# A hybrid mixer's weights split on ScalarE and VectorE instead of by an accumulating DMA, and a longer weight ring in the direct pairs

## The chip, the cores and the metric

One core of a Trainium2 chip runs the whole program. The metric is the device time in microseconds (us) of one execution. A kernel is timed in several executions, and the median counts. One further execution was taken with the hardware profiler, and all rows below are of that one.

## The reference

Two decoder layers over 512 tokens of 1024 features, all in float32. Every layer is a SwiGLU network, a token mixer and another SwiGLU network, each added to the stream; a last RMSNorm ends it. Cut to what the change touches:

```python
def swiglu_ffn(x, g, w_in, w_out):
    h = rms_norm(x, g)
    gate, up = jnp.split(h @ w_in, 2, axis=-1)
    return (jax.nn.silu(gate) * up) @ w_out

def retention_dilated_mixer(x, norm_g, w_in, ret_gn, w_out):      # layer 0: the hybrid mixer
    h = rms_norm(x, norm_g)
    rq, rk, rv, rg, dq, dk, dv = jnp.split(h @ w_in, cuts, axis=-1)
    rq, rk = rotary(rq), rotary(rk)
    ret = merge_heads(head_group_norm(retention_chunkwise(rq, rk, rv), ret_gn)) * jax.nn.silu(rg)
    dil = merge_heads(dilated_attention(rotary(dq), rotary(dk), dv))
    return jnp.concatenate([ret, dil], axis=-1) @ w_out
```

Layer 1 has a stick-breaking attention in the mixer's place. The four networks have an inner width of 2816.

## The kernel before

**Numbers in two parts.** TensorE multiplies in the type fp32r, which rounds. To keep float32's accuracy every operand is cut into a rounded part hi and a remainder lo, and each product is three matmuls (`mm3`, L221): hi by hi, hi by lo, lo by hi. A weight *unit* is a tile of 128 x 1024 floats (512 KB). It comes by DMA into a raw tile (`wraw`), is cut, and hi and lo go into two tiles of a ring (`whl`). One unit of a projection feeds 24 matmuls of 512 columns.

**Two ways to cut a unit.** `weight` (L150) takes hi as a ScalarE cast and lo as a VectorE subtraction, raw minus hi (`split`, L227). `weight_dma` (L196) has ScalarE write minus hi into lo, and then GpSimd's queue issues a DMA that reads the same weights from memory a second time and adds them into lo (`minus_hi`, L191); ScalarE also makes hi. `unit` (L215) takes the second way for the weights in `BY_DMA`, which are all the input weights of the hybrid mixer; the first gate unit alone goes through `weight`. The stick-breaking mixer's weights were cut during earlier stages and kept in memory (`weight_cut`).

**Who sets the order.** Matmuls are chained in the order in which the program calls them (`ordered`, L119). For the other engines a scheduler places each instruction by priority; `tc.high_priority` moves some ahead. Each engine and each DMA queue then works strictly in its order. A tile from a ring can be written once its last reader is done.

**The network.** `ffn_seven` (L551) computes four feature blocks plainly, the *direct pairs*: a gate unit and an up unit each, eight units, of which those of blocks 2 and 3 go through `weight_dma`. Then nine `quad`s follow with seven products in place of eight (L501). Their sums and forms are made by VectorE and ScalarE. `give` sets which slots of memory a role turns through: in the direct pairs before, `wraw` has 4 and `whl` 6, three units; the slots `ext` join for the quads (L598).

**The hybrid mixer** (`hybrid`, L863). Four gate projections come first, into three accumulators in turn. The row factor r of the norm is made from the sum of squares by a matmul `po`, two ScalarE functions and three VectorE steps (`norm_r`, L290); four transposes on TensorE bring it to token order (`token_r`, L623), after the third gate projection before the change. Then a stream of steps (`stream`, L910) makes queries and keys, eight pairs of units, and values, four pairs. A query or key tile is rotated by four VectorE operations (`rot_steps`, L752), cut in two, and moved by DMAs into the layout of the scores (`pack_q`, `pack_k`). Between the steps of the stream the sixteen heads take turns: scores of the next head (`begin`), some steps, then `attend` (L719), whose result ScalarE and VectorE bring out of the bank `po`. After every second retention head `ret_norm` (L809) squares it and a matmul with `bd` sums it. In the mixer before, `wraw` has 2 slots and `whl` 8, four units.

Of the kernel before, what the change touches and what calls it, by code (L numbers as in the profile page):

```python
# [35 lines left out]
def trunk(ctx: ExitStack, tc: tile.TileContext, a: dict, out: bass.AP):  # L36
    nc = tc.nc
# [150 lines left out]

    BY_DMA = ["hyb_" + n for n in ("g", "rq", "rk", "rv", "dq", "dk", "dv")]

    def minus_hi(lo, src, raw):  # L191
# [23 lines left out]
    def unit(key, cols):  # L215
        if key in cut:
            return weight_cut(key, cols)
        src = centred.get(key, array_unit(key))
        return weight_dma(src, cols) if key[0] in BY_DMA else weight(src, cols)

# [330 lines left out]
    def ffn_seven(rms, wd, wq, gcol, first=None):  # L551
# [4 lines left out]
        for i, n in enumerate(("T3", "T1", "T4", "B11", "T2", "B22", "B21")):  # L556
            give(**{"f" + n: forms[2 * i:2 * i + 2]})
        give(uq=late + old[:4])
        uqs = []
        for f in range(DIRECT):  # L560
# [34 lines left out]
            if f == DIRECT - 1:  # L595
                fm = normed_forms(rr, gcol, late[DIRECT // 2 + 1:], forms[12:] + forms[10:12])
        ring = oldest("whl")
        give(wraw=ext[:1] + oldest("wraw") + old[6:], p3=ext[1:2], whl=ring[:4] + ext[2:] + ring[4:] + old[4:6])  # L598
        for q in range((FC - DIRECT) // 2):
# [118 lines left out]

    def attend(v, p, e, banks, o):  # L719

        po = PS("po")
        for j in range(NB):
            b, at = WHERE[e, j]
            n = size(j)
            st = v[j][:, 2 * (p % 2) + e, :, :].rearrange("p a d -> p (a d)")
            for c in range(2):
                mm(po[:, SEQ - n:], st, banks[b][:, c, at:at + n], start=j == 0 and c == 0,
                   stop=j == NB - 1 and c == 1, skip_group_check=True)
        t = T()
        rows, oth = slice(e * DH, e * DH + DH), slice(DH - e * DH, 2 * DH - e * DH)  # L730
        nc.scalar.copy(out=t[rows, :], in_=po[oth, :])
        nc.vector.tensor_add(out=o[rows, :], in0=po[rows, :], in1=t[rows, :])

# [129 lines left out]
    def hybrid(ss, gcol_next):  # L863
        order["on"] = True
        mixer_roles()
        raws, ring = oldest("wraw"), oldest("whl")
        give(wraw=raws[2:], whl=ring + raws[:2])
        gates, held = [], []
        for p in range(4):
            held.append(ACC())  # L870
            if p == 0:
                w = weight(a["hyb_g"][0], D)
                proj_tile(None, held[-1], w)
            else:
                proj_tile(("hyb_g", p), held[-1])
            if p == 0:
                epsr = hpool.tile([P, SEQ], F32, tag="ss", name=nm("epsr"))
                r = norm_r(ss, epsr)
            if p < 2:
                continue  # L880
            if p == 2:
                rtm = token_r(r)
                rtm2 = cpool.tile([P, NB], F32, tag="rtm2", name="rtm2")
                nc.vector.tensor_mul(out=rtm2, in0=rtm, in1=rtm)
                act_set(SILU)
            for ps in held:
                g = T()
                nc.vector.tensor_mul(out=g, in0=ps, in1=r)
                if len(gates) % 2 == 0:
                    gg = B((P, 2, SEQ), F32, f"o{6 + len(gates) // 2}")  # L890
                gates.append(gg[:, len(gates) % 2, :])
                func(gates[-1], g, AF.Silu)
            held = []
# [47 lines left out]
        for h in range(16):  # L941
# [9 lines left out]
            if e == 0:  # L951
                o = T(tag="oo")
            attend(vs[p // 2], p, e, ready.pop(h), o)
            if e == 0:
# [6 lines left out]
        for _ in flow.steps:  # L961
            pass
        raws, ring = oldest("wraw"), oldest("whl")
        give(wraw=raws + ring[:2], whl=ring[2:])
        ss = out_second("hyb_ob", outs, gcol_next)
# [302 lines left out]
```

## Time and profile before

| | us |
|---|---|
| median of 3 runs | 1937.59 |
| lowest, highest | 1937.23, 1941.17 |
| the profiled execution, device time | 1935.8 |
| its span, first to last instruction | 1934.1 |
| TensorE busy with matmuls, in the span | 1908.1 |

The profiled execution's device time is 1.7 us more than its span. In the rows, PE is TensorE's matmuls, PEld its weight loads, DVE VectorE, ACT ScalarE, POOL GpSimd and SP the queue of the plain DMAs. A matmul's listed duration is longer than its share of the engine, because matmuls overlap: the distance from one start to the next tells the pace. An idle time in brackets stands with who ended it; where that engine had long been done, it was another.

### The profile page before, as it was taken

How to read it: one execution, taken by the hardware profiler on the slowest of the kernel's cores; microseconds unless marked ns; L12 is line 12 of the kernel's file. 1: busy time of each engine (PE TensorE's matmuls, PEld its weight loads, DVE VectorE, ACT ScalarE, POOL GpSimd, SP SyncE). 2: the span in 40 equal slices, each digit the busy share in tenths (PEclk: the TensorE clock that was granted, in tenths of full speed). 3: DMA queues.
4: the chain of work that ended last, by engine and by line, in shares of the span. 5: the costliest groups of instructions: out<-in, count | busy, mean ns of one | idle time of the engine just before them, and what ended most of it. 6: DMA issues, size and time to landing. Idle time of an engine off the chain costs nothing.

```text
span 1934.1 us, 30592 instructions
## 1 busy us (share of the span) xinstructions
PE 1908.1 (99%) x11936; PEld 1724.9 (89%) x11936; DVE 1299.5 (67%) x1854; ACT 1100.2 (57%) x1558; POOL 193.7 (10%) x317
## 2 busy tenths in 40 slices
PE   9999999999999999999999999999999999999998
PEld 7999988787888899998779999888888888999887
DVE  8967755346777876674478677443888879676534
ACT  6666733545775666673356567333666656666523
POOL 0111000212100111100001110000222201111000
PEclk9999999999999999999999999999999999999999
DMA  8776677799843767768866766777555447867333
GB/s 240 184 201 163 149 265 246 204 256 216 186 121 100 183 166 191 189 181 277 278 168 178 192 169 155 248 239 237 160 184 151 149 139 178 202 162 179 101 95 118
DMA packets 112448, 357.82 MB, mean 185 GB/s; under 512 B 13744, under 2 KB 15408, under 8 KB 112304
## 3 DMA queue, kind: packets, MB, share of 16 engines
q1 hardware_dynamic: 90992, 278.54, 44.0%
q0 software_dynamic: 21168, 77.08, 22.8%
q8 instruction: 93, 1.52, 0.3%
q14 instruction: 51, 0.42, 0.1%
q10 hardware_dynamic: 144, 0.26, 0.0%
HBM read 297.11 MB, written 37.75 MB: 173 GB/s over the span
## 4 chain that ended last, share of the span: by engine, by line
PE 84%; DMA 6%; issue 5%; DVE 3%; ACT 1%; POOL 0%; SPq 0%; DVEq 0%; POOLq 0%; ACTq 0%
PE att L126 43%; PE acc L126 39%; PE po L126 2%; DMA wraw<-hyb_rq 1%; DMA whl<-wd 1%; DVE whl L229 1%; DMA cut_sb_k<-whl 1%; DMA o<-rot_k 1%; DVE h L260 1%; DMA whl<-wq 0%; PE att L129 0%; DMA qk<-ah 0%; ACT whl L193 0%; DMA cut_sb_v<-whl 0%; DMA wraw<-sb_q 0%
## 5 line engine op out<-in xcount | busy, mean ns | idle before, releaser
L228 ACT CAST whl<-wraw 128x1024 fp32r<-128x1024 f32 (+4 forms) x284 | 277.7, 984 | 404.3 <-PE acc L126 158.5
L229 DVE TENSOR_TENSOR whl<-wraw,whl 128x1024 fp32r<-128x1024 f32 (+4 forms) x284 | 322.8, 1141 | 248.1 <-ACT whl L228 206.0
L126 PE MATMUL acc<-u,whl 128*128 128x512 f32 (+1 forms) x2244 | 484.4, 377 | 1.8 <-DVE whl L229 1.8
L126 PEld LDWEIGHTS acc<-u,whl 128*128 128x128 f32 x2244 | 403.1, 188 | 81.6 <-DVE whl L229 4.3
L126 PE MATMUL att<-fT,whl 128*128 128x256 f32 x3456 | 426.4, 283 | 0.0
L126 PEld LDWEIGHTS att<-fT,whl 128*128 128x128 f32 x3456 | 420.1, 192 | 0.3
L126 PE MATMUL att<-fB,whl 128*128 128x256 f32 x2592 | 323.0, 283 | 0.0
L126 PEld LDWEIGHTS att<-fB,whl 128*128 128x128 f32 x2592 | 316.3, 192 | 0.2 <-DMA whl<-wq 0.2
L126 PE MATMUL acc<-h,whl 128*128 128x512 f32 x1056 | 257.4, 394 | 4.2 <-DMA whl<-wd 3.0
L126 PEld LDWEIGHTS acc<-h,whl 128*128 128x128 f32 x1056 | 196.4, 188 | 49.9 <-DMA whl<-wd 4.6
L479 ACT CAST whl<-wraw 128x1024 fp32r<-128x1024 f32 x104 | 109.1, 1049 | 110.1 <-PE att L126 108.9
L481 POOL DMA_DIRECT2D whl<-wq x104 | 90.1, 866 | 643.6 <-ACT whl L480 277.7
L480 ACT ACTIVATE whl<-whl 128x1024 fp32r<-128x1024 f32 x104 | 110.2, 1060 | 3.0
L229 DVE TENSOR_TENSOR whl<-p,whl 128x1024 fp32r<-128x1024 f32 x36 | 44.1, 1224 | 84.7 <-ACT whl L228 84.7
L126 PE MATMUL att<-h,whl 128*128 128x512 f32 x384 | 93.0, 393 | 0.0
L126 PEld LDWEIGHTS att<-h,whl 128*128 128x128 f32 x384 | 72.3, 189 | 16.7 <-issue 1.4
L126 PE MATMUL acc<-whl,h 128*128 128x256 f32 x576 | 74.4, 285 | 0.0
L126 PEld LDWEIGHTS acc<-whl,h 128*128 128x128 f32 x576 | 72.4, 192 | 1.0
L329 DVE SCALAR_TENSOR_TENSOR x<-acc,x 128x512 f32<-128x512 f32 (+1 forms) x34 | 22.4, 658 | 68.9 <-PE acc L126 68.9
L973 POOL TENSOR_SCALAR_AFFINE_SELECT t<-t 128x128 f32<-128x128 f32 x128 | 45.9, 380 | 187.3 <-DVE t L990 121.3
L201 ACT CAST whl<-wraw 128x1024 fp32r<-128x1024 f32 x43 | 44.9, 1047 | 32.6 <-PE acc L126 16.5
L108 ACT ACTIVATE t<-t 128x512 f32<-128x512 f32 (+1 forms) x100 | 57.2, 590 | 5.1 <-DVE t L537 2.8
(184 smaller groups left out, 2256.6 us busy)
## 6 DMA issues: line engine op xcount, KB each, us to landing
wraw<-wq SPq DMA_DIRECT2D x144, 512.0 KB, 5.3
whl<-wq POOLq DMA_DIRECT2D x104, 512.0 KB, 6.8
wraw<-f_out SPq DMA_DIRECT2D x68, 448.0 KB, 4.4
wraw<-f_out SPq DMA_DIRECT2D x34, 512.0 KB, 4.5
wraw<-wd SPq DMA_DIRECT2D x30, 512.0 KB, 4.1
whl<-wd POOLq DMA_DIRECT2D x16, 512.0 KB, 8.0
cut_sb_q<-whl SPq DMA_DIRECT2D x16, 512.0 KB, 3.5
cut_sb_k<-whl SPq DMA_DIRECT2D x16, 512.0 KB, 5.3
```

Source lines behind the costliest of these rows:

```text
L108: r = nc.scalar.activation(out=o, in_=i, func=f, **kw)
L126: return ordered(nc.tensor.matmul(*args, **kw))
L201: nc.scalar.copy(out=hi, in_=raw[:, :cols])
L228: nc.scalar.copy(out=hi, in_=src)
L229: nc.vector.tensor_tensor(out=lo, in0=src, in1=f32(hi), op=ALU.subtract)
L260: nc.vector.scalar_tensor_tensor(out=lo, in0=x[c], scalar=g, in1=f32(hi), op0=ALU.mult, op1=ALU.subtract)
L329: nc.vector.scalar_tensor_tensor(out=x[d][:, sl], in0=ps[:, sl], scalar=0.5, in1=x[d][:, sl], op0=ALU.mult, op1=ALU.add)
L479: nc.scalar.copy(out=hi, in_=raw)
L480: nc.scalar.mul(out=lo, in_=f32(hi), mul=-1.0)
L481: nc.gpsimd.dma_start(lo, src, accum_op=ALU.add)
L973: nc.gpsimd.affine_select(out=t[:, at:at + P], in_=t[:, at:at + P], pattern=[[1, P]], compare_op=ALU.is_gt, fill=0.0, base=0, channel_mult ...
```

## The change

All units of the hybrid mixer go through `weight`; `BY_DMA` is gone. The mixer no longer takes two raw slots for the ring, so `wraw` has 4 slots there and `whl` 6, three units. The slots `ext` join at the start of `ffn_seven`, so in the direct pairs `wraw` has 5 and `whl` 8, four units; blocks 2 and 3 still use `weight_dma`. `token_r` and the first gates' functions come after the second gate projection. The two operations that bring out a head's result in the hybrid mixer get a higher priority.

```diff
-    BY_DMA = ["hyb_" + n for n in ("g", "rq", "rk", "rv", "dq", "dk", "dv")]
...
     def unit(key, cols):
         if key in cut:
             return weight_cut(key, cols)
-        src = centred.get(key, array_unit(key))
-        return weight_dma(src, cols) if key[0] in BY_DMA else weight(src, cols)
+        return weight(centred.get(key, array_unit(key)), cols)
...
-        give(uq=late + old[:4])
+        give(uq=late + old[:4], wraw=oldest("wraw") + ext[:1], whl=oldest("whl") + ext[2:])
...
-        ring = oldest("whl")
-        give(wraw=ext[:1] + oldest("wraw") + old[6:], p3=ext[1:2], whl=ring[:4] + ext[2:] + ring[4:] + old[4:6])
+        give(wraw=oldest("wraw") + old[6:], p3=ext[1:2], whl=oldest("whl") + old[4:6])
...
-    def attend(v, p, e, banks, o):
+    def attend(v, p, e, banks, o, soon=0):
...
-        nc.scalar.copy(out=t[rows, :], in_=po[oth, :])
-        nc.vector.tensor_add(out=o[rows, :], in0=po[rows, :], in1=t[rows, :])
+        with tc.high_priority(offset=soon):
+            nc.scalar.copy(out=t[rows, :], in_=po[oth, :])
+            nc.vector.tensor_add(out=o[rows, :], in0=po[rows, :], in1=t[rows, :])
...
     def hybrid(ss, gcol_next):
         order["on"] = True
         mixer_roles()
-        raws, ring = oldest("wraw"), oldest("whl")
-        give(wraw=raws[2:], whl=ring + raws[:2])
...
-            if p < 2:
+            if p == 0:
                 continue
-            if p == 2:
+            if p == 1:
                 rtm = token_r(r)
...
-            attend(vs[p // 2], p, e, ready.pop(h), o)
+            attend(vs[p // 2], p, e, ready.pop(h), o, SOON)
...
-        raws, ring = oldest("wraw"), oldest("whl")
-        give(wraw=raws + ring[:2], whl=ring[2:])
         ss = out_second("hyb_ob", outs, gcol_next)
```

**ScalarE at the start of the hybrid mixer.** Each row is an instruction, out<-in; `x_83` and `h_3518` belong to the last of the eight chunks of the stream, `po` holds the mean square, and the two rows from it are the logarithm and the exponential on the way to r. Before:

```order
L267 ACTIVATE t_3566<-x_83 128x512
L259 ACTIVATE h_3518<-x_83,gains 128x512
L193 ACTIVATE whl_3669<-wraw_3667 128x1024
L201 CAST whl_3668<-wraw_3667 128x1024
L201 CAST whl_3712<-wraw_3711 128x1024
L193 ACTIVATE whl_3713<-wraw_3711 128x1024
L108 ACTIVATE t_3571<-po_3569,eps_n 128x512
L108 ACTIVATE t_3573<-t_3571 128x512
```

and now:

```order
L264 ACTIVATE t_3566<-x_83 128x512
L256 ACTIVATE h_3518<-x_83,gains 128x512
L225 CAST whl_3666<-wraw_3665 128x1024
L108 ACTIVATE t_3571<-po_3569,eps_n 128x512
L108 ACTIVATE t_3573<-t_3571 128x512
```

Before, the fourth gate unit (`wraw_3667`) and the first query unit (`wraw_3711`) stand ahead of the logarithm with two instructions each; now the fourth gate unit's cast alone does.

**VectorE at the first query's and key's rotation.** `acc` is the projection, `o_536` and `o_545` the tables of the rotation, `sp` and `ah` the tiles from which the DMAs move. Before:

```order
L757 STREAM_SHUFFLE tp_3742<-acc_3710 128x512
L759 TENSOR_TENSOR tp_3744<-acc_3710,o_536_3708 128x512
L760 TENSOR_TENSOR tp_3742<-tp_3742,o_536_3708 128x512
L761 TENSOR_TENSOR tp_3744<-tp_3744,tp_3742 128x512
L681 SCALAR_TENSOR_TENSOR sp_3748<-tp_3744,sp_3748 128x512
```

and now:

```order
L754 STREAM_SHUFFLE tp_3738<-acc_3707 128x512
L756 TENSOR_TENSOR tp_3740<-acc_3707,o_536_3705 128x512
L757 TENSOR_TENSOR tp_3738<-tp_3738,o_536_3705 128x512
L226 TENSOR_TENSOR whl_3834<-wraw_3832,whl_3833 128x1024
L758 TENSOR_TENSOR tp_3740<-tp_3740,tp_3738 128x512
L677 SCALAR_TENSOR_TENSOR sp_3744<-tp_3740,sp_3744 128x512
```

A weight's subtraction stands between the third and the fourth step; it does so in 10 of the 16 rotations. GpSimd's queue has 27 DMAs fewer.

**ScalarE in the second network's direct pairs.** `wraw_6333` before and `wraw_6306` now are the gate unit of block 2, the first of `weight_dma`. Before:

```order
L228 CAST whl_6271<-wraw_6270 128x1024
L108 ACTIVATE t_6242<-po_6240,eps_n 128x512
L201 CAST whl_6334<-wraw_6333 128x1024
L108 ACTIVATE t_6244<-t_6242 128x512
L102 ACT_TABLE_LOAD
L193 ACTIVATE whl_6335<-wraw_6333 128x1024
```

and now:

```order
L199 CAST whl_6307<-wraw_6306 128x1024
L191 ACTIVATE whl_6308<-wraw_6306 128x1024
L108 ACTIVATE t_6215<-po_6213,eps_n 128x512
L199 CAST whl_6314<-wraw_6313 128x1024
L108 ACTIVATE t_6217<-t_6215 128x512
L102 ACT_TABLE_LOAD
```

Minus hi, behind which GpSimd's DMA waits, stands ahead of the logarithm now; before it stood behind the load of the function table. On VectorE the addition `p3` of the first quad moves ahead of the three steps to r in this network.

## Rows read from the trace of the kernel before

**Rows 1.** The page, busy us (share of span) xinstructions of three engines
```profile
PE 1908.1 (99%) x11936; PEld 1724.9 (89%) x11936; DVE 1299.5 (67%) x1854; ACT 1100.2 (57%) x1558; POOL 193.7 (10%) x317
```

**Rows 2.** Windows, stretches of the hybrid mixer and, last, the stick-breaking mixer
```profile
core 0: us, PE busy (x) PEld busy (x) DVE busy (x) ACT busy (x) POOL busy (x), PEclk, DMA share, GB/s
355.00:405.00 50.00, 46.45 (x249) 39.16 (x248) 15.29 (x27) 26.85 (x33) 10.36 (x11) 1.00 0.95 242
405.00:460.00 55.00, 50.47 (x270) 43.77 (x269) 28.65 (x53) 27.65 (x43) 12.55 (x23) 0.94 0.94 237
460.00:603.00 143.00, 142.86 (x814) 124.83 (x812) 107.17 (x231) 100.70 (x208) 15.96 (x26) 1.00 0.63 153
...
1326.00:1557.00 231.00, 230.34 (x1339) 204.38 (x1339) 186.07 (x388) 139.94 (x280) 45.85 (x128) 1.00 0.56 171
```

**Rows 3.** Timeline of TensorE, start of the mixer: start, us, instruction, [idle before <-releaser]
```profile
353.79 5.60 PE L126 MATMUL acc<-h,whl 128*128 128x512 f32 x24
359.23 1.02 PE L126 MATMUL po<-ss,ones_ms 128*128 128x512 f32 x2
...
372.54 0.63 PE L129 MATMUL att<-ident,r 128*128 128x128 f32 x4 [0.79 <-PE acc L126]
373.31 16.78 PE L126 MATMUL acc<-h,whl 128*128 128x512 f32 x72
...
403.90 0.41 PE L126 MATMUL att<-qk,qk 128*128 128x384 f32 x1 [2.30 <-DMA qk<-ah]
```

**Rows 4.** Timelines of ScalarE, then VectorE, the way to r
```profile
366.55 1.05 ACT L201 CAST whl<-wraw 128x1024 fp32r<-128x1024 f32 x1 [6.32 <-DMA wraw<-hyb_rq]
...
368.46 0.67 ACT L108 ACTIVATE t<-po,eps_n 128x512 f32<-128x512 f32 x1
...
371.75 0.69 DVE L250 SCALAR_TENSOR_TENSOR r<-t,t 128x512 f32<-128x512 f32 x1
```

**Rows 5.** Timeline of TensorE, the first group norm's matmul
```profile
445.46 2.07 PE L126 MATMUL att<-t,bd 128*128 128x512 f32 x2 [4.53 <-DMA wraw<-hyb_dq]
```

**Rows 6.** Timeline of ScalarE ahead of that matmul
```profile
441.43 1.06 ACT L193 ACTIVATE whl<-wraw 128x1024 fp32r<-128x1024 f32 x1 [4.00 <-DMA wraw<-hyb_rk]
...
444.78 0.63 ACT L812 ACTIVATE t<-oo 128x512 f32<-128x512 f32 x1 [0.76 <-DVE oo L732]
```

**Rows 7.** Windows, the 5 us behind that wait
```profile
446.00:451.00 5.00, 5.00 (x18) 3.82 (x17) 2.89 (x6) 4.17 (x7) 1.89 (x4) 0.53 0.99 220
```

**Rows 8.** TensorE's waits in the whole span: us in total, times, longest us
```profile
PE acc L126 <- DMA whl<-wd: 3.0, 3, 1.1
PE acc L126 <- DVE whl L229: 2.4, 6, 0.6
```

**Rows 9.** Timelines of GpSimd, then VectorE, second network: accumulating DMA, `p3`'s addition
```profile
636.59 0.86 POOL L194 DMA_DIRECT2D whl<-wd  x1 [101.70 <-ACT whl L193]
...
640.10 1.22 DVE L507 TENSOR_TENSOR p<-wraw,wraw 128x1024 f32<-128x1024 f32 x1 [0.23 <-DMA wraw<-wq]
```

**Rows 10.** Groups of instructions, the page and the hybrid mixer's (354 to 604 us)
```profile
L228 ACT CAST whl<-wraw 128x1024 fp32r<-128x1024 f32 (+4 forms) x284 | 277.7, 984 | 404.3 <-PE acc L126 158.5
L229 DVE TENSOR_TENSOR whl<-wraw,whl 128x1024 fp32r<-128x1024 f32 (+4 forms) x284 | 322.8, 1141 | 248.1 <-ACT whl L228 206.0
...
L193 ACT ACTIVATE whl<-wraw 128x1024 fp32r<-128x1024 f32 x26 | 27.4, 1054 | 11.0 <-DMA wraw<-hyb_rk 7.1 <-PE acc L126 2.6 <-DMA wraw<-hyb_g 1.3
```

**Rows 11.** DMA, 355 to 460, then 1330 to 1550 us: queue's share; median us to landing
```profile
q0 software_dynamic: 2448, 8.91, 46.0%
qk<-ah SPq DMA_DIRECT2D x12, 128.0 KB, 7.0
...
qk<-misc SPq DMA_DIRECT2D x64, 128.0 KB, 3.3
```

**Rows 12.** Timelines of VectorE and GpSimd, two instructions that overlap
```profile
438.20 0.90 DVE L681 SCALAR_TENSOR_TENSOR ah<-tp,ah 128x512 fp32r<-128x512 f32 x1
438.52 0.85 POOL L805 TENSOR_SCALAR_AFFINE_SELECT ah<-ah 128x256 fp32r<-128x256 f32 x1
```

## The prediction

> **What bounds the kernel.** I read the page first: TensorE is busy in 1908.1 of the span's 1934.1 us, VectorE in 1299.5, ScalarE in 1100.2 [rows 1]. The change leaves every matmul in place, so it can gain only where TensorE stands idle, runs at the lower clock or starts matmuls at less than its pace, and all of the idle time together is 26 us. Then I cut the hybrid mixer into windows [rows 2]. In its first 105 us TensorE misses 3.55 us in the first 50 and 4.53 in the next 55, while the DMA engines are busy 0.95 and 0.94; in the 143 us after that it misses 0.14. Last, I looked in TensorE's timeline and in its table of waits for each loss, and followed each back on the engine that released it.
>
> Two things stand out. In the first 105 us GpSimd's queue, the one of the accumulating DMAs, takes 46.0% of the sixteen engines' time [rows 11]; and ScalarE's minus hi, 1.054 us each [rows 10], waits for raw weights there while other work is queued behind it. For 0.2%, 3.9 us, is about what a measurement of this kernel tells from no change, I take 1933.7 and 1941.5 as the bounds of "same".
>
> **What the losses are.** The pace comes from the first gate projection: 24 matmuls from 353.79 to 359.23, 5.44 us, 0.227 each [rows 3].
>
> (a) The way to r. From 353.79 to 373.31 TensorE makes three projections (3 x 5.44 = 16.32), two matmuls to `po` (0.45) and the transposes (373.31 − 372.54 = 0.77): 17.54 of 19.52 us, so 1.98 are lost [rows 3]. The mean square is in `po` near 360.3, but ScalarE starts the logarithm only at 368.46, because the first query unit's cast stands ahead and waited 6.32 us for its DMA; r is complete at 372.44 [rows 4], 3.98 us after the logarithm began. Now that unit no longer stands ahead. The logarithm can start near 360.4 and r is there near 364.4. The transposes, now one projection earlier, are due at 353.79 + 2 x 5.44 + 0.45 = 365.1. The margin is 0.7 us: I take the whole 1.98. The bound below is a gain of nothing, if the fourth gate unit, whose cast is still ahead, lands late.
>
> (b) The first scores wait 2.30 us for the moves that lay out the queries and keys [rows 3]. These moves land after a median of 7.0 us here, and after 3.3 in the stick-breaking mixer [rows 11], whose DMA share is 0.56 [rows 2]. One move that is 3 us quicker covers the wait, also against a subtraction of 1.14 us ahead of it. Taken: 2.30. Bound below: nothing.
>
> (c) The first group norm's matmul waits 4.53 us [rows 5]. The row names a DMA, but what comes last is the squaring at 444.78, behind an addition of a head's result, behind a copy that stood on ScalarE behind minus hi and hi of a unit. That minus hi waited 4.00 us for raw weights and began at 441.43 [rows 6]. The change removes minus hi and the second reading of the weights, and gives copy and addition a higher priority. Taken: 4.53; bound below 0.5, what stays if the copy still has a cast of 0.98 [rows 10] and a late unit ahead.
>
> (d) For the 5 us behind that wait the granted clock is 0.53, the lower of the two levels (1.2 GHz), after TensorE had stood idle [rows 7]. No other window here shows less than 0.94 [rows 2]. Without the idle time I expect 1.00: 5 x (1 − 0.53) = 2.35 us. It goes with (c) or not at all.
>
> (e) In the direct pairs TensorE waits three times for an accumulating DMA of `w_in`, 3.0 us in all [rows 8]. In the second network that DMA was issued at 636.59 [rows 9]; its minus hi stood behind the logarithm and the load of the function table. With four units in the ring minus hi comes ahead of the logarithm. The three steps to r and the additions that use it end with `r` after that, so the DMA leaves some 8 us earlier against waits of at most 1.1. Taken: 3.0; bound below: nothing.
>
> **What is removed elsewhere.** 27 times minus hi on ScalarE, 27 x 1.054 = 28 us, and 27 DMAs of 512 KB. ScalarE is busy 100.70 of 143 us in the mixer's second part [rows 2], where TensorE waits for it nowhere: no further gain is counted.
>
> **What is added.** 27 subtractions of 1.141 us on VectorE [rows 10], 30.8 us. In the second part of the mixer VectorE's load goes from 107.17 of 143 us, 75%, by about ten units to 118.6, 83%. The nearest row is the stick-breaking mixer, with VectorE at 186.07 of 231 us, 81%, and TensorE missing 0.66 [rows 2]. So the load in itself costs nothing; what could is the order. Ten of sixteen rotations get a subtraction ahead of their last step and reach the scores 1.14 us later. The cover is the quicker moves: 7.0 against 3.3 us [rows 11]. I charge one uncovered subtraction, 1.14 us, for the first head, where queries have no lead. Bounds: 0, and ten, 11.4.
>
> The mixer's ring goes from four units to three. A unit is used for 5.44 us [rows 3]; with three in the ring a slot is free for 2 x 5.44 = 10.9 us ahead of its next use, and cast and subtraction take 0.98 + 1.14 = 2.1 [rows 10]. Cost nothing, with 8.8 us for queueing; that cover gone, the third rival says what follows.
>
> In network 2 the addition for the first quad (1.22 us, at 640.10, held 0.23 by its DMA [rows 9]) is moved ahead of the three VectorE steps to r. If its data come no earlier than before, r would be some 6 us later. But its DMAs go on the plain queue, and the raw ring has one slot more, so that I expect them before r's functions are done. Cost nothing; bound 6.
>
> One rule speaks against the change. VectorE and GpSimd disturb each other in the trace: a scaled subtraction with two inputs in memory on chip takes 0.90 us while a GpSimd selection runs, which itself takes 0.85 [rows 12]; the like operation toward r takes 0.69 [rows 4]. By these rows 27 more such operations cost at most 27 x 0.21 = 5.7 us of VectorE time, off TensorE's path, so the sum keeps zero. The Trainium skill (SBUF — State Buffer, § Who interferes with whom) says that a VectorE instruction with two inputs there and a GpSimd instruction that reads there lock each other out wholly, the later one waiting. By that rule the 27 subtractions could wait for a whole GpSimd operation each, which the row prices at 0.85: an estimate of 23 us of VectorE time, which would bring the third rival near. The row shows 0.21 of 0.85, so the wait there was not whole.
>
> **The sum.** 1.98 + 2.30 + 4.53 + 2.35 + 3.0 = 14.16 less 1.14 is 13.02. The profiled execution took 1935.8 us, 1.8 below the median of 1937.59, so it becomes 1922.8, and the median, by the same gain, **1924.6**. Small changes of (b) and (e) make this case 1920 to 1929.
>
> **Rivals.**
>
> *The transfers stay late.* If (b) and (e) are set by something else than GpSimd's queue and minus hi, 2.3 + 3.0 remain: 1929.9. For it: the waits of (e) keep their accumulating DMAs, and a longer ring alone doesn't issue them if ScalarE's order leaves them late; in that part the change would not do what it says. Against it: the order shows minus hi ahead of the logarithm in network 2.
>
> *Given back.* The nine other subtractions inside rotations are uncovered too: 9 x 1.14 = 10.3, 1934.9. For it: VectorE's chain to the scores gets longer in ten of sixteen steps. Against it: 0.66 us in 231 at 81% load [rows 2].
>
> *Slower.* VectorE becomes the bound of the mixer's three-unit ring: a unit's subtraction stands in VectorE's queue behind a rotation's wait for its projection, and that projection's successor waits for the unit. Each of the 27 units then comes a subtraction late, 27 x 1.14 = 30.8 in place of 1.14: 1954.3. It decides from 16.9 us of loss, 0.63 per unit, on. For it: TensorE already waits six times, 2.4 us, for a subtraction of this kind [rows 8]. Against it: 0.4 us each is below that point, and the slot is free 10.9 us ahead. The Trainium skill (Perfetto Trace Analysis, § Optimizing Scalar/DVE Operations) has work go from VectorE to ScalarE where VectorE is the saturated one; this change goes the other way, and 83% is not saturated by the stick-breaking mixer's row.
>
> *More than the terms.* The six waits of 2.4 us [rows 8] shrink too, and so do losses without a row of their own in the mixer's first 105 us: 3 to 6 us more, near 1920.
>
> **Chances.** The forecast (1920 to 1929) 0.60; late transfers 0.18; given back 0.11; slower 0.05; more 0.06. The range, 1919 to 1933, leaves out given back and slower, 0.16. Faster are the forecast, late transfers and more, 0.84; same 0.11; slower 0.05. All cases but two lie on one side, because the losses that go have been seen in rows, while the costs would have to come out of cover that similar work has elsewhere.
>
> **What would show it.** Right: no idle time ahead of the transposes of r, of the first scores and of the first `bd` matmul; a granted clock of 1.00 in the windows behind; a DMA share clearly below 0.95 and no GpSimd queue in 355 to 460; moves landing in 3 to 5 us; no wait for a DMA of `w_in` in TensorE's waits; ScalarE down by some 28 us and VectorE up by some 31. Wrong: waits of `acc` for the subtraction of `split` once per unit; scores waiting for moves after a late fourth rotation step; transposes waiting for r; r's VectorE steps in network 2 behind the addition's DMA.

## The result, and the profile after

The changed kernel took 1929.49 us (median of 6 runs, 1925.55 to 1932.61) against 1939.19 for the kernel before in the same 12 runs. The ratio is 0.9946, with a 95% interval of 0.9926 to 0.9965: 10.5 us faster, between 6.8 and 14.3. The forecast was 13.0 us. Its time, 1924.6, started from the median of the first three executions before, 1937.59; with all six that median is 1939.19.

The profiled execution of the changed kernel is the slowest of its six, 1932.61 us; that of the kernel before, 1935.8, is shorter than its median. The two profiles are therefore only 3.2 us apart, and part of what the later one loses outside the mixer may be that execution's own.

The page's line of busy times, of the changed kernel:

```profile
PE 1906.7 (99%) x11936; PEld 1723.5 (89%) x11936; DVE 1324.9 (69%) x1881; ACT 1074.3 (56%) x1531; POOL 170.8 (9%) x290
```

ScalarE has 25.9 us less than in [rows 1], VectorE 25.4 more. The windows of the hybrid mixer answer to [rows 2]; its first gate projection starts 3.9 us later here, since the first network took longer, of which more below:

```profile
core 0: us, PE busy (x) PEld busy (x) DVE busy (x) ACT busy (x) POOL busy (x), PEclk, DMA share, GB/s
355.00:405.00 50.00, 50.00 (x270) 43.15 (x269) 25.56 (x38) 19.34 (x25) 2.55 (x2) 1.00 0.51 156
405.00:460.00 55.00, 55.00 (x306) 48.16 (x305) 42.89 (x69) 24.32 (x42) 8.76 (x20) 1.00 0.58 166
460.00:603.00 143.00, 143.00 (x811) 124.88 (x811) 115.45 (x236) 90.71 (x196) 5.34 (x12) 1.00 0.41 114
```

TensorE misses nothing in the whole mixer, where it missed 3.55, 4.53 and 0.14 us. The granted clock is 1.00 throughout, and the DMA share fell from 0.95 and 0.94 to 0.51 and 0.58. VectorE works 115.45 of 143 us, 81%. TensorE's timeline there, which answers to [rows 3] and [rows 5] (the rows of the first projection, the transposes of r, the first scores, the first group norm):

```profile
357.72 5.60 PE L126 MATMUL acc<-h,whl 128*128 128x512 f32 x24
...
369.50 0.60 PE L129 MATMUL att<-ident,r 128*128 128x128 f32 x4
...
403.23 0.34 PE L126 MATMUL att<-qk,qk 128*128 128x384 f32 x1
...
440.03 1.02 PE L126 MATMUL att<-t,bd 128*128 128x512 f32 x2
```

No bracket stands behind any of them: the three waits are gone. ScalarE's timeline shows why for the first and the third, beside [rows 4] and [rows 6]:

```profile
363.18 1.05 ACT L225 CAST whl<-wraw 128x1024 fp32r<-128x1024 f32 x1 [3.28 <-issue]
364.22 0.69 ACT L108 ACTIVATE t<-po,eps_n 128x512 f32<-128x512 f32 x1
...
435.87 0.58 ACT L728 COPY t<-po 64x512 f32<-64x512 f32 x1 [0.74 <-PE po L126]
437.21 0.63 ACT L809 ACTIVATE t<-oo 128x512 f32<-128x512 f32 x1 [0.76 <-DVE oo L729]
```

The logarithm starts 6.50 us after the first gate projection's start (357.72 to 364.22), where it took 14.67 (353.79 to 368.46). The copy of the head's result now waits for TensorE alone, and the squaring is done 2 us before it is needed. The DMA view of 355 to 460 us has no GpSimd queue any more, and the median landing of the keys' moves from `ah`, 7.0 us in [rows 11], is 2.3; the queries' moves from `sp` took 8.4 before and take 5.0:

```profile
q1 hardware_dynamic: 6056, 16.80, 54.1%
...
qk<-sp SPq DMA_DIRECT2D x16, 128.0 KB, 5.0
...
qk<-ah SPq DMA_DIRECT2D x12, 128.0 KB, 2.3
```

Elsewhere TensorE waits more than before. Its table of waits, the first five rows, beside [rows 8]:

```profile
PE att L126 <- ACT t L510: 3.8, 6, 0.9
PE acc L126 <- DVE whl L226: 3.8, 7, 0.8
PE po L126 <- DVE t L1080: 1.6, 1, 1.6
PE att L126 <- DVE t L527: 1.6, 2, 0.9
PE acc L126 <- ACT whl L225: 1.5, 4, 0.5
```

The waits for an accumulating DMA of `wd` (the `w_in` of the direct pairs), 3.0 us, are gone too. But `att <- t L510` and `t L527` are new, 5.4 us: these are products of the `quad`s that wait for a bank to be read. They lie in the first quads of three of the four networks (the first, the second and the last), where the kernel before lost nothing. The waits for a cast or a subtraction, 5.3 us, are all but 0.6 in the output projection at the end of the second network: 4.7 us there, 1.8 before, and 3.0 in the kernel with late transposes (below), whose second network is the same. That spread shows how much they vary; no run ties them to the change. A window of 50 to 150 us, the first network's quads, of the kernel before:

```profile
50.00:150.00 100.00, 100.00 (x825) 99.53 (x824) 78.97 (x90) 63.91 (x74) 11.25 (x13) 1.00 0.73 187
```

and of the changed kernel:

```profile
50.00:150.00 100.00, 96.87 (x789) 95.44 (x789) 75.00 (x85) 61.27 (x73) 11.25 (x13) 1.00 0.73 184
```

So the mixer gave what was forecast, and part of it was lost in a place that the prediction had put down as a gain. The experiments first take the change apart, and then look for the edit that does this.

### The profile page after: what moved, and what is told of

It reads as the page before. It is cut to its first block, busy times and chain, and to the rows that moved or that the text cites. A ratio compares the mean times of both kernels' runs of the same rounds, so it can differ in the third digit from the quotient of the medians.

```text
span 1930.8 us, 30512 instructions
## 1 busy us (share of the span) xinstructions
PE 1906.7 (99%) x11936; PEld 1723.5 (89%) x11936; DVE 1324.9 (69%) x1881; ACT 1074.3 (56%) x1531; POOL 170.8 (9%) x290
## 4 chain that ended last, share of the span: by engine, by line
PE 80%; DVE 8%; DMA 7%; issue 3%; ACT 1%; SPq 0%; POOL 0%; DVEq 0%; ACTq 0%; POOLq 0%
PE acc L126 39%; PE att L126 38%; DMA wraw<-wq 2%; PE po L126 2%; DVE whl L226 2%; DMA cut_sb_k<-whl 1%; DMA wraw<-sb_q 1%; DVE tt L451 1%; DVE fT L226 1%; DVE h L257 1%; DVE tf L434 1%; DMA wraw<-f_out 1%; DMA whl<-wq 1%; PE att L129 0%; ACT whl L225 0%
## 5 line engine op out<-in xcount | busy, mean ns | idle before, releaser
L225 ACT CAST whl<-wraw 128x1024 fp32r<-128x1024 f32 (+4 forms) x311 | 305.3, 989 | 425.8 <-PE acc L126 176.4
L226 DVE TENSOR_TENSOR whl<-wraw,whl 128x1024 fp32r<-128x1024 f32 (+4 forms) x311 | 355.9, 1150 | 249.4 <-ACT whl L225 206.0
L476 ACT CAST whl<-wraw 128x1024 fp32r<-128x1024 f32 x104 | 109.1, 1049 | 93.5 <-PE att L126 91.7
L504 DVE TENSOR_TENSOR p<-wraw,wraw 128x1024 f32<-128x1024 f32 x36 | 44.2, 1226 | 48.4 <-DMA wraw<-wq 44.1
```

Of the source, the lines that this page charges most:

```text
L225: nc.scalar.copy(out=hi, in_=src)
L226: nc.vector.tensor_tensor(out=lo, in0=src, in1=f32(hi), op=ALU.subtract)
L476: nc.scalar.copy(out=hi, in_=raw)
L504: nc.vector.tensor_add(out=p3, in0=a11, in1=a21)
```

## The experiments

Times below are ratios to the kernel before, run beside each kernel on the same chip, with their 95% intervals; a thousandth is 1.94 us.

**The changed kernel with the old ring in the direct pairs.**

```diff
-        give(uq=late + old[:4], wraw=oldest("wraw") + ext[:1], whl=oldest("whl") + ext[2:])
+        give(uq=late + old[:4])
...
-        give(wraw=oldest("wraw") + old[6:], p3=ext[1:2], whl=oldest("whl") + old[4:6])
+        ring = oldest("whl")
+        give(wraw=ext[:1] + oldest("wraw") + old[6:], p3=ext[1:2], whl=ring[:4] + ext[2:] + ring[4:] + old[4:6])
```

> The changed kernel, but with the three-unit ring of before in the direct pairs (and the slots given to the quads in the old order). Theory: the parts of the change add up; the mixer keeps its gain, the three waits for an accumulating DMA of w_in come back, 3.0 us in all, and the 5 to 9 us that the changed kernel's profile shows as new losses in the quads vary from execution to execution, with no tie to the ring. Then some 7 us faster than before (5 to 9), 3 us slower than the changed kernel. Rival: the new order of the slots makes the raw weights of the quads late and costs those 5 to 9 us; then this kernel shows none of them, as the profile of before does, and is 10 to 14 us faster than before, so faster than the changed kernel.

Measured: 1925.08 us, 0.9927 (0.9914 to 0.9941), 14.2 us faster than before. That is what the rival said, and 4 us more than the changed kernel's ratio gives, though the two intervals overlap. Its window and waits:

```profile
50.00:150.00 100.00, 99.37 (x808) 98.49 (x809) 77.75 (x88) 63.49 (x74) 11.25 (x13) 1.00 0.76 189
```

```profile
PE acc L126 <- DMA whl<-wd: 4.5, 4, 1.4
...
PE att L126 <- DMA whl<-wd: 1.4, 1, 1.4
```

The waits for the accumulating DMA are back, 5.9 us with those of `att`, and yet the kernel is no slower: the quads lose 0.63 us in this window in place of 3.13, and the direct pairs ahead of them 4.34 us up to 50 us in place of 2.52.

**The ring alone,** in the kernel before: the same lines as above, the other way round.

> The kernel before with the ring of the direct pairs alone, four units. Theory: the three waits for the accumulating DMA go and nothing else moves: 3 us faster than before (1 to 4). Rival (the order of the slots costs the quads): TensorE loses 4 to 5 us between 50 and 350 us, as in the changed kernel's profile, and some 4 us more in the other networks, so that the kernel is 2 to 6 us slower than before although the three waits are gone.

Measured: 1.0007 (0.9992 to 1.0021). A gain of 3 us would be 0.9985, which the interval excludes; the rival's 2 to 6 us are not reached at its middle either, which is 1.4 us slower, though its upper end is 4.1 us slower. The profile has the rival's mechanism: TensorE is busy 97.39 of the 100 us from 50 to 150. No row of its waits names `wd`. What the ring takes from one wait it gives to others.

**The new cuts alone,** in the kernel before.

```diff
-    BY_DMA = ["hyb_" + n for n in ("g", "rq", "rk", "rv", "dq", "dk", "dv")]
+    BY_DMA = []
```

> The kernel before with the hybrid mixer's weights through weight (cast and subtraction), and nothing else: two raw slots, a ring of four units, transposes after the third gate projection, no priority for a head's result. Theory: the second reading of the weights and minus hi are what made the mixer lose its time, so the 4.5 us ahead of the first group norm's matmul, the half clock behind it, the 2.3 us ahead of the first scores and most of the 2.0 us around r go with this edit alone: 9 to 11 us faster than before. Rival: the raw slots are what counts; with two, a unit is loaded only when the unit two before it has been cut, cast and subtraction in a row, and TensorE waits for raw weights; then less than 5 us faster.

Measured: 0.9938 (0.9921 to 0.9954), 12.0 us faster. One line does as much as the whole change. In its windows

```profile
355.00:460.00 105.00, 105.00 (x573) 91.14 (x572) 71.56 (x111) 45.51 (x67) 11.33 (x22) 1.00 0.58 168
460.00:603.00 143.00, 141.73 (x805) 123.97 (x804) 112.92 (x232) 90.05 (x196) 5.35 (x12) 1.00 0.40 114
```

the first 105 us of the mixer are without a loss and at the full clock, with two raw slots and with the transposes where they were. The rival of the raw slots falls. ScalarE's order ahead of the logarithm is in part the old one here: the first query unit's cast still stands in front and still waits for its DMA, but these weights land in time:

```profile
362.38 1.05 ACT L228 CAST whl<-wraw 128x1024 fp32r<-128x1024 f32 x1 [3.42 <-DMA wraw<-hyb_rq]
363.33 0.68 ACT L108 ACTIVATE t<-po,eps_n 128x512 f32<-128x512 f32 x1
```

The logarithm starts 7.89 us after the first gate projection, which began at 355.44, and that is soon enough. What is left, 1.27 us, is one wait in its table, for the addition of a head's result:

```profile
PE po L126 <- DVE oo L732: 1.3, 1, 1.3
```

**The transposes after the third projection again,** in the changed kernel.

```diff
-            if p == 0:
+            if p < 2:
                 continue
-            if p == 1:
+            if p == 2:
                 rtm = token_r(r)
```

> The changed kernel with the transposes of r after the third gate projection again. Theory: r comes early because the logarithm does not wait for a query unit's cast any more, and the place of the transposes adds nothing: within 1.5 us of the changed kernel, 8 to 11 us faster than before, no idle time ahead of the transposes. Rival: the earlier place carries the gain of 2 us at the mixer's start: 2 us or more slower than the changed kernel. Its first network is the changed kernel's, instruction by instruction, so that its profile also shows whether the loss of 4.5 us there (50 to 350 us) recurs.

Measured: 0.9942 (0.9926 to 0.9958), against 0.9946. The place of the transposes is worth nothing that can be measured; r comes early without it. Its first network, which is the changed kernel's, misses 2.62 us from 50 to 150, against 3.13: the loss there recurs.

**Which half of the ring.** Two kernels, each the changed one with half of the edit. Five raw slots and three units:

```diff
-        give(uq=late + old[:4], wraw=oldest("wraw") + ext[:1], whl=oldest("whl") + ext[2:])
+        give(uq=late + old[:4], wraw=oldest("wraw") + ext[:1])
...
-        give(wraw=oldest("wraw") + old[6:], p3=ext[1:2], whl=oldest("whl") + old[4:6])
+        ring = oldest("whl")
+        give(wraw=oldest("wraw") + old[6:], p3=ext[1:2], whl=ring[:4] + ext[2:] + ring[4:] + old[4:6])
```

> The changed kernel with half of the ring's edit: five raw slots in the direct pairs, but three units, the two other slots joining only for the quads in the place they had before. Theory A (the fifth raw slot is at fault: it was the free slot into which the first quad's weights came early, and its use in the direct pairs shifts which slot each quad's weights take): TensorE loses 3 to 5 us between 50 and 150 us, as in the changed kernel, the waits for the accumulating DMA of w_in stay, and it is the slowest of these, near the changed kernel or 1 to 3 us slower, some 9 us faster than before. Theory B (the fourth unit is at fault: it moves the cuts of the first quad ahead on ScalarE and VectorE, and what they are ahead of comes late): no loss there, some 14 us faster than before, like the changed kernel with the old ring. Theory C (neither: the first quads' weights come at a time of their own, and what the direct pairs gain is waited for there): losses between 50 and 150 us equal to what the waits ahead of them lack.

And four raw slots and four units:

```diff
-        give(uq=late + old[:4], wraw=oldest("wraw") + ext[:1], whl=oldest("whl") + ext[2:])
+        give(uq=late + old[:4], whl=oldest("whl") + ext[2:])
...
-        give(wraw=oldest("wraw") + old[6:], p3=ext[1:2], whl=oldest("whl") + old[4:6])
+        give(wraw=ext[:1] + oldest("wraw") + old[6:], p3=ext[1:2], whl=oldest("whl") + old[4:6])
```

> The other half: four units in the direct pairs, four raw slots, the fifth raw slot joining for the quads at the head of their list as before. Theory A: the waits for the accumulating DMA go and nothing is lost in the quads: 3 to 6 us faster than the changed kernel with the old ring, 17 to 20 us faster than before. Theory B: the losses of the changed kernel in the first quads, 3 to 5 us between 50 and 150 us and as much in the other networks, 9 to 11 us faster than before. Theory C: the sum of the losses up to 150 us stays at 8 to 9 us, as with either ring, and the time is within 2 us of the changed kernel with the old ring.

Measured: 0.9918 (0.9904 to 0.9931) with the raw slot, 0.9931 (0.9919 to 0.9944) with the fourth unit. The times alone hardly part them; the windows do. With the fifth raw slot:

```profile
50.00:150.00 100.00, 99.91 (x820) 99.17 (x819) 78.60 (x88) 63.63 (x75) 11.26 (x13) 1.00 0.74 188
```

With the fourth unit:

```profile
50.00:150.00 100.00, 96.38 (x781) 94.62 (x780) 74.53 (x86) 61.22 (x72) 11.26 (x13) 1.00 0.72 180
```

Theory B: the loss of 3 us belongs to the fourth unit. Theory A falls with the first window, and theory C, that the quads only wait for what was gained ahead of them, too: up to 50 us the two kernels lose 2.58 and 3.12 us, so the one that loses less there also loses less after it. Where the loss comes from stands in ScalarE's order in the first network. This is the piece of the difference, with + for the kernel with four units and − for the one with three; `wraw_470` holds the sum of two raw tiles for the first quad's second product, `p_75_478` the sum for its first, `wraw_472` the raw tile for its third:

```
-L225 CAST whl_541<-wraw_470 128x1024
 L225 CAST fT_95_548<-tt_545 128x512
 L225 CAST fT_96_551<-tt_545 128x512
-L476 CAST whl_480<-wraw_472 128x1024
-L477 ACTIVATE whl_481<-whl_480 128x1024
+L225 CAST whl_489<-p_75_478 128x1024
 L225 CAST fB_119_737<-tf_500 128x512
 L225 CAST fT_109_658<-tt_581 128x512
 L225 CAST fT_110_661<-tt_581 128x512
 L225 CAST fB_118_734<-tf_499 128x512
-L225 CAST whl_489<-p_75_478 128x1024
+L225 CAST whl_541<-wraw_470 128x1024
```

With three units the two slots `ext[2:]` are empty while the direct pairs run, and the second product's unit is cut into them early. With four units the direct pairs use those slots, and this cut has to wait until one of their units is done. When it happens can be read on ScalarE, with three units (the raw-slot kernel):

```profile
42.24 1.04 ACT L225 CAST whl<-wraw 128x1024 fp32r<-128x1024 f32 x1
```

and with four:

```profile
51.59 1.04 ACT L225 CAST whl<-wraw 128x1024 fp32r<-128x1024 f32 x1
```

It is 9.35 us later. Its raw slot is held until it is cut and added to, and the sixth raw tile of the quads, next on the plain queue, goes into that slot. This DMA on the plain queue with three units:

```profile
48.19 0.33 SPq L502 DMA_DIRECT2D wraw<-wq  x1
```

and with four:

```profile
54.08 0.33 SPq L502 DMA_DIRECT2D wraw<-wq  x1
```

It leaves 5.89 us later, and the seventh and eighth behind it; the twelfth still leaves at 76.97 in place of 74.20. TensorE comes to these quads at the same time in both (53.11 and 53.06 us) and, with four units, waits for a subtraction and then for a copy on ScalarE:

```profile
68.26 5.78 PE L126 MATMUL att<-fB,whl 128*128 128x256 f32 x46 [0.41 <-DVE whl L226]
...
81.11 1.10 PE L126 MATMUL att<-fT,whl 128*128 128x256 f32 x7 [1.32 <-ACT t L510]
```

The copy stands on ScalarE behind two cuts and two functions, the first of which waits for VectorE; and on VectorE the addition for the third quad was held for its raw weights. With three units and with four:

```profile
70.61 1.22 DVE L504 TENSOR_TENSOR p<-wraw,wraw 128x1024 f32<-128x1024 f32 x1 [0.69 <-DMA wraw<-wq]
```

```profile
73.39 1.23 DVE L504 TENSOR_TENSOR p<-wraw,wraw 128x1024 f32<-128x1024 f32 x1 [2.31 <-DMA wraw<-wq]
```

Over all profiles taken, TensorE misses 2.6 to 3.6 us from 50 to 150 in the four kernels with four units in the first network (changed, ring alone, late transposes, this one), and 0 to 1.1 in the nine with three units and `weight_dma` for block 3. That the fourth unit is at fault in this window is shown by the four kernels with either number of raw slots: with four and with five, three units lose 0.63 and 0.09 us and four units 3.62 and 3.13. That it works through the late cut is read from these rows, and no run puts the cut back early while keeping four units. The waits before 50 us differ too: up to 150 us together the four kernels lose 5.0 to 6.7 us and the nine 2.2 to 6.2, so what the fourth unit costs in the whole is less sure than what it costs in this window.

**No accumulating DMA in the direct pairs.** The other way to be rid of the waits for `wd`: the old ring, and block 2's two units through `weight`; in a second kernel block 3's as well (`f < 4`).

```diff
-                w2 = [(weight if f < 2 else weight_dma)(wd[i], D) for i in (f, DIRECT + f)]
+                w2 = [(weight if f < 3 else weight_dma)(wd[i], D) for i in (f, DIRECT + f)]
```

> The changed kernel with the old ring in the direct pairs, and there block 2's two units through weight as well (cast and subtraction), so that block 3's alone have an accumulating DMA. Theory: what holds for the mixer holds here, half of the waits for the accumulating DMA of w_in (5.9 us in the old ring's profile) go, and VectorE, which has two subtractions of 1.14 us more in a stretch of 57 us at 83%, covers them: 2 to 3 us faster than with the old ring alone, some 16 us faster than before. Rival: VectorE is the bound of the direct pairs, since the norm's forms for the quads are made there; the quads wait for their forms, 2 x 1.14 us in each of four networks: up to 9 us slower than with the old ring alone.

> As the one before, with block 3's units through weight too: no accumulating DMA is left in the direct pairs. Theory: all waits for it go, 4 to 6 us faster than with the old ring alone, some 19 us faster than before. Rival: four subtractions, 4.6 us, more on VectorE in a stretch of 57 us where it is busy 47: it becomes the bound, and TensorE waits for a subtraction or for the forms of the first quad, more than it gains: slower than with the old ring alone by up to 4 x 4 x 1.14 = 18 us.

Measured: 1919.07 us, 0.9893 (0.9878 to 0.9908) with block 2, 1920.09 us, 0.9896 (0.9882 to 0.9909) with both. The first is 20.8 us faster than before and some 10 us faster than the changed kernel by their ratios, whose intervals don't meet. With block 2 the first network's quads lose nothing and no wait for `wd` stands in the table:

```profile
50.00:150.00 100.00, 100.00 (x828) 99.65 (x827) 78.92 (x89) 62.82 (x73) 11.71 (x14) 1.00 0.71 180
```

Two subtractions remove all the waits, not half as the theory said: block 3's two DMAs, alone on GpSimd's queue there, come in time. VectorE takes them, 53.16 of 57 us from 603 to 660 where it was 51.46 with the old ring. The next two units bring nothing more, and with them the first quads lose 1.58 us.

**One removed load put back at a time.** All three on the kernel with the old ring, whose ratio was 0.9927: 27 DMAs of 512 KB on GpSimd's queue, or 27 times minus hi on ScalarE, or, as a test of the forecast's cover, every subtraction of the mixer's units done twice.

```diff
+            junk = dram.tile([P, 1024], F32, tag=nm("junk"), name=nm("junk"))
+            nc.gpsimd.dma_start(junk[:, :cols], f32(lo))
```

> The changed kernel with the old ring in the direct pairs (a_oldring), and after each of the hybrid mixer's 27 subtractions a DMA of 512 KB on GpSimd's queue that copies lo to a place in memory where nobody reads it: the traffic of the removed DMAs without minus hi on ScalarE and without anybody that waits for it. Theory (the traffic itself made the moves and the raw weights late): the DMA share in the first 105 us of the mixer rises from 0.55 to 0.9, the moves land after 6 us or more instead of 4, the first scores wait for them again, 2.3 us, and the whole is 2 to 8 us slower than a_oldring. Rival (what was late came from ScalarE's order, from casts and minus hi that waited in front of the logarithm and the copy): within 1.5 us of a_oldring.

```diff
+            nc.scalar.mul(out=lo, in_=raw[:, :cols], mul=-1.0)
         split(hi, lo, raw[:, :cols])
```

> The changed kernel with the old ring in the direct pairs (a_oldring), and in each of the hybrid mixer's 27 units ScalarE writes minus hi into lo ahead of the cast, as before, which the subtraction then overwrites: the 28 us of ScalarE come back, the DMAs do not. Theory: ScalarE has room (busy 91 of 143 us in the mixer's second part), and a unit is early enough when its data are; within 1.5 us of a_oldring. Rival: minus hi in ScalarE's order was what made the copy of a head's result late; the 4.5 us ahead of the first group norm's matmul come back, and 2 us of half clock behind it.

```diff
         split(hi, lo, raw[:, :cols])
+            nc.vector.tensor_tensor(out=lo, in0=raw[:, :cols], in1=f32(hi), op=ALU.subtract)
```

> The changed kernel with the old ring in the direct pairs (a_oldring), and each of the mixer's 27 subtractions done twice: 30.8 us more on VectorE, which then is busy some 127 of the 143 us in the mixer's second part, 89%. Theory (as the prediction had it: the added VectorE work is hidden and the cover is not used up): less than 3 us slower than a_oldring. Rival (the case on the other side: VectorE is close to being the bound of the ring of three units): 10 to 30 us slower, TensorE waiting for a subtraction once per unit.

Measured: 0.9923 (0.9909 to 0.9937) with the DMAs, 0.9926 (0.9912 to 0.9939) with minus hi: neither costs anything by itself. With the traffic the moves from `ah` land after a median of 4.7 us from 355 to 460, where it was 2.7 with the old ring alone, and the first scores don't wait. The DMA share was 0.77 there and not the 0.9 that was expected: the traffic was lighter than that which it stands for. Its queue there, beside [rows 11]:

```profile
q0 software_dynamic: 2446, 8.91, 21.2%
```

The same 8.91 MB took 46.0% of the sixteen engines before. So the theory of traffic alone is refuted only for traffic of this weight; whether the accumulating DMAs' full weight, or it together with minus hi in front of other work, made the waits of before, stays open. The two were not put back together. Minus hi, too, was put back as work and not in its old place: this kernel keeps the priority of a head's result, and no minus hi stands ahead of the copy before the first group norm, which waits for TensorE alone:

```profile
435.17 0.58 ACT L733 COPY t<-po 64x512 f32<-64x512 f32 x1 [0.74 <-PE po L126]
```

So the rival, minus hi in front of that copy, was not tested here.

With doubled subtractions: 1931.04 us, 0.9954 (0.9942 to 0.9967), some 5 us slower than with the old ring. Its window and the wait that most of it is:

```profile
456.00:599.00 143.00, 139.44 (x794) 121.41 (x793) 127.42 (x248) 90.90 (x195) 5.55 (x13) 1.00 0.40 111
```

```profile
PE att L126 <- ACT t L814: 2.7, 1, 2.7
```

VectorE at 89% of this stretch lets TensorE miss 3.56 us, 2.72 of them at one group norm. It is not a subtraction late once per unit: 5 us over 27 units are 0.2 each. Theory's bound of 3 us was too low, the rival's 10 too high.

**Without the priority,** on the kernel with the old ring: `SOON` left out of the call of `attend`.

> The changed kernel with the old ring in the direct pairs (a_oldring) and without the higher priority for a head's result. Theory: the wait ahead of the first group norm's matmul went with minus hi and the DMAs, as in the kernel before with the new cuts alone, and the priority is worth the one wait of 1.3 us for a head's result that was left there: 0 to 2 us slower than a_oldring. Rival: the priority is what keeps the copy ahead of the casts; then 4 to 7 us slower.

Measured: 1928.71 us, 0.9942 (0.9927 to 0.9956), some 3 us slower by the ratios, whose intervals overlap; that is above what the theory allowed and below the rival. The first group norm does not wait. The loss is in another place:

```profile
PE po L126 <- DVE oo L730: 1.9, 1, 1.9
```

```profile
456.00:599.00 143.00, 141.12 (x796) 123.53 (x795) 115.18 (x235) 90.42 (x195) 6.88 (x15) 0.99 0.40 110
```

A product at 528.85 us waits 1.88 for the addition of a head's result: its copy on ScalarE was done at 519.46, but VectorE comes to the addition only at 528.03, behind the next head's softmax steps and a rotation. Then the granted clock is at the lower level, which the window right behind it shows:

```profile
528.90:532.00 3.10, 3.10 (x12) 2.92 (x13) 1.54 (x2) 1.07 (x2) 0.00 (x0) 0.50 0.41 96
```

These 3.1 us alone cost another 3.10 x (1 − 0.50) = 1.55.

## Why the prediction was right, and where not

- **(a) The way to r, 1.98:** gone, but only some 1.1 of it was r. At the pace of 0.227 the third matmul of the second gate projection was due at 359.69 + 2 x 0.227 = 360.14; it started at 361.04, 0.90 later, since the accumulating DMA of its unit had not landed. The prediction's sum over three projections took this wait for one for r. (The bracket is shorter, since it counts from the listed end of the matmul before.)

```profile
359.69 1.03 PE L126 MATMUL acc<-h,whl 128*128 128x512 f32 x2
361.04 10.72 PE L126 MATMUL acc<-h,whl 128*128 128x512 f32 x46 [0.32 <-DMA whl<-hyb_g]
```

The late-transposes kernel shows that the earlier transposes were not needed for the gain, and the new cuts alone that the query unit's cast may stand ahead of the logarithm if its weights land in time.
- **(b) The first scores, 2.30:** gone. The moves from `ah` land after 2.3 us, better than the 3 to 5 that were expected, those from `sp` after 5.0.
- **(c) and (d), the group norm and the half clock, 4.53 and 2.35:** gone, with the new cuts alone, so without the priority. The prediction put the priority beside the cuts in (c); it does nothing there, and is worth perhaps 3 us, with overlapping intervals, at a later head that the prediction did not name.
- **Together,** (a) to (d) were 11.16 us. The profiled mixer lost 8.22 us of idle time and the half clock before, and loses nothing now; the kernel with the old ring is 14.2 us faster (11.4 to 16.7 by its interval), the new cuts alone 12.0.
- **The added subtractions, 1.14 charged:** they cost nothing visible. The price of 1.141 is a mean over five forms, and those of the mixer are listed with 1.235 each; VectorE's busy time rose by 25.4 us in this profile and by 29.9 with the old ring, against 30.8 expected. VectorE's load of 81% in the mixer's second part agrees with the 83% worked out, and with the stick-breaking mixer's row that was taken as the measure. The cover is not endless: a second dose, 29.9 us more on VectorE, costs about 5. Of the slower rival, one subtraction late per unit, nothing shows. The six waits for a subtraction of [rows 8], 2.4 us, did not shrink: they are 3.8, and none of them in the mixer.
- **VectorE beside GpSimd, nothing charged:** right about the cost, but [rows 12] don't show that the wait was not whole. Just before, the same selection on a tile of the same size took 0.40 us, and beside the subtraction 0.85, so GpSimd's instruction lost 0.45 there while VectorE's lost 0.21:

```profile
438.16 0.40 POOL L805 TENSOR_SCALAR_AFFINE_SELECT c<-c 128x256 fp32r<-128x256 f32 x1
```

- **The ring of three in the mixer, nothing charged:** right; TensorE misses nothing there.
- **(e) The direct pairs, 3.0: the step that failed.** The waits went, and minus hi moved ahead as the order had shown, but "bound below: nothing" was wrong. The ring alone measures 1.0007 (0.9992 to 1.0021), and by the ratios of the changed kernel with and without it the ring costs 0.9946 − 0.9927 = 0.0019, 3.7 us, though these two intervals overlap. The prediction asked what the four units release and not what they take: the slots `ext[2:]` stood empty in the direct pairs, and the first quad's cut was already using them.
- **`p3`'s addition in network 2, nothing charged:** the cost came out, the reason did not. The prediction expected the raw weights before r's functions were done; they came after, and VectorE stood 8.03 us with r's three steps behind the addition:

```profile
629.49 1.23 DVE L504 TENSOR_TENSOR p<-wraw,wraw 128x1024 f32<-128x1024 f32 x1 [8.03 <-DMA wraw<-wq]
...
632.08 0.69 DVE L247 SCALAR_TENSOR_TENSOR r<-t,t 128x512 f32<-128x512 f32 x1
```

Here r was complete 9.35 us after the logarithm began (623.42), where it took 4.33 before. This is the sign of being wrong that the prediction had named, and close to its bound of 6. It is the fourth unit's doing: the four kernels with four units held this addition for 6.3 to 8.0 us, the others for 0.4 at most. That it cost little in the direct pairs is luck: TensorE misses 0.62 of the 57 us from 603 to 660, none of it for r. Whether it has a part in the 0.86 us that the second network's first quads lose is not shown.

The forecast of 13.0 us was too high by 2.5, within the interval of the result (6.8 to 14.3): 3.0 of it was no gain, and the loss that came in its place was not seen. The 1.14 that were charged and not paid hid part of that: without both, 11.16 remain. The time lies beside the case "the transfers stay late" (1929.9) and just outside the likeliest one (1920 to 1929), but that case has another reason: (b) did not stay, and in (e) the transfers did come earlier. Of the distance to the forecast time, 4.9 us, 1.6 lie in the kernel before, whose median rose from 1937.59 to 1939.19 with three more executions.

## What to carry to other kernels

A slot that stands empty in one stage may be the next stage's head start: before a ring is made longer, look in the order for who writes those slots now, and at which time. A wait that costs 3 us can then be replaced by one of the same size in a stage that had no loss. The same wait went without that price by removing the transfer (two units cut on VectorE) instead of starting it earlier, and the kernel so made is the fastest here, 0.9893 (0.9878 to 0.9908).

## What had not been expected

An accumulating DMA on GpSimd's queue took 2.2 times the DMA engines' time of a plain one for the same bytes in the same stretch: 46.0% against 21.2% for 8.91 MB from 355 to 460 us. They differ in direction too (from memory into the chip's tiles, and from tiles to memory), so what of it is the adding is not shown. And the length of one idle time does not tell whether TensorE's clock falls: the granted clock was 0.50, the lower level, behind a wait of 1.88 us (without the priority), and stayed at 1.00 behind one of 2.72 at a group norm (doubled subtractions):

```profile
508.40:512.00 3.60, 3.56 (x18) 2.42 (x18) 3.57 (x7) 1.85 (x4) 0.00 (x0) 1.00 0.91 199
```

Where it fell, it added at least 1.55 us to the wait of 1.88, and the 2.35 of (d) to one of 4.53; the prediction counted it from the row and was right to tie it to its own wait.
